# A hybrid decoder layer by Strassen-like products: attention's projection by columns, stores on ACT's queue, split weights stored later, and one more set of products by seven

## The chip, the cores and the metric

One Trainium2 chip, of which the kernel uses 1 core. The metric is the time of the launch on the device, in microseconds; lower is better. The core has five engines that work side by side, each through a queue of its own: PE (matmuls), DVE (vector), ACT (scalar, activations), POOL (GpSimd) and SP (here it only issues DMAs). Matrices lie in SBUF, sums of products in PSUM, of which a bank holds 128 x 512 numbers.

## The reference

One step of one layer: a sliding-window attention branch and a gated linear attention (GLA) branch in parallel, merged by gates, then an output projection and a layer norm. There are 2048 prompt tokens and 8 x 8 sample tokens; the model's width is 1024. All is float32.

```python
z = jnp.einsum('btd,dn->btn', x, w_in)
q, k, v, g_att, gq, gk, gv, g_gla, g_lr, r_att, r_gla = jnp.split(z, SPLIT_POINTS, axis=-1)
o_att = swa_prompt(q, k, v, attn_sink, rel_table)          # windows of 128, softmax with sinks
log_a = jax.nn.log_sigmoid(g_lr @ w_gk_up + b_gk) / GATE_NORMALIZER
o_gla, S = gla(gq * (GLA_HK ** -0.5), gk, gv, log_a, s0)   # recurrent state, chunk by chunk
o_gla = o_gla * lax.rsqrt(mean(o_gla ** 2) + EPS) * gla_norm_w
h_att = (o_att * silu(g_att)) @ w_pa
h_gla = (o_gla * silu(g_gla)) @ w_pg
merged = sigmoid(r_att) * h_att + sigmoid(r_gla) * h_gla
x = layer_norm(DN_ALPHA * x + merged @ w_o, ln_g, ln_b)
```

Besides y the kernel returns the last keys and values and the GLA states, for prompt and sample. It computes `sigmoid` by `tanh`, and the halves that this needs are folded into later steps.

## The kernel before, in words

**Float32 by parts.** A float32 product goes through PE as three products of a high and a low part: `wh*xh`, `wh*xl` and `wl*xh` (lines 1291, 1292, 1293). The parts are made by `split` (line 140): ACT casts the high part (L142), DVE subtracts it from the source to get the low part (L143).

**Products by seven.** The 2112 tokens are three thirds s of 704, and a third is two halves t of 352 columns. For a pair of 256 output columns (p) and the two halves of the depth (k), the four blocks of the output (two column halves c by two token halves t) come from seven block products in place of eight (Strassen's scheme in Winograd's form). The products have numbers, in the order 1, 7, 6, 4, 5, 2, 3 (`ORDER`); a product is one *group* of 12 matmuls of 352 columns. For it there are seven operands of x (`Ops`: x1 to x7, sums and differences by `mix`, parts by `make`) and seven weights (`w_make`). Where a weight's block is used for the first time, POOL adds and subtracts the raw blocks (L338) for weights 7, 6 and 3. Products 1, 7 and 6 are copied from PSUM by ACT into `a` tiles (L374, L378), and DVE adds these to products 4, 5 and 2 (L383, L389, L395).

**Sets.** The main loop runs over groups, set by set: x0, x1, a0, u0, x2, a1, u1, a2, u2. An x set is the input projection of a third (17 column pairs) and the two gates r (8 pairs, `RA_`, `RG_`). An a set is attention's projection of a third (`PA_`, weights `w_pa`, depth 512, so that a group is 6 matmuls), a u set is GLA's (`PG_`, weights `w_pg`). The sets named in `PLAIN` go by eight plain products, in 16 groups for two pairs, the others by seven, in 14. In a plain set two pairs have four PSUM banks (`role`), one for each pair and token half.

**Side work.** `tick` starts work of the attention, of GLA and of setup at given ticks of the main loop; its matmuls stand between the groups. Setup makes the relative bias (`setup0` to `setup5`); `gla_norm` has two small steps on POOL (L1071, L1072).

**Weights.** Ahead of group g the loop issues the load of raw weights of group g + 8 into `ws` tiles (`w_first`, L311, on SP), the load of kept weights of g + 5 (`w_kept`, L318), makes the weight of g + 4 (`w_make`, into `wp` tiles, of which there are six), and loads the gates `part` for g + 2 (L175). In x0 the made weights 7, 6, 5, 3 are stored to HBM (L361, `wk`), and x1 and x2 load them instead of making them anew.

**Sinks.** What is done with an output tile: `keep_sink` stores it (L187), `silu_sink` (L202) and `tanh_sink` (L212) apply an activation first, `gated_sink` of an a set multiplies it by its gate `part` on DVE (L219) and stores it (L221), `merge_sink` of a u set does the same (L227) and adds it to that in HBM by POOL's accumulating DMA (L229). All the other stores and loads are issued by SP.

**What sets the order.** PE's order is the program's. The other engines' orders are set when the kernel is built, largely by the order in the program; each engine then waits for what its next instruction needs, and so does SP with each DMA. Small tiles come from pools with a fixed number of buffers (`mtile`: `xb` 16, `a` 8, `fin` 10, `ws` 9, `wp` 6), and an instruction that writes a buffer waits until the earlier use is over.

Of the kernel before, what the change touches and what calls it, by code (L numbers as in the profile page):

```python
# [12 lines left out]
F32 = mybir.dt.float32  # L13
# [37 lines left out]
EIGHT = [(c, k, t) for c in range(2) for k in range(2) for t in range(2)]  # L51
PLAIN = ("a0", "a1", "a2", "u0", "u1", "u2")
KEPT = (7, 6, 5, 3)
# [4 lines left out]
def kernel(ctx, tc, io):  # L58
# [22 lines left out]
    def mtile(tag, dt=F32, name=None):  # L81
        n, bufs = {"xb": (4 * T, 16), "a": (T, 8), "fin": (T, 10), "ws": (512, 9), "wp": (D, 6)}[tag]
        pool = px if tag == "xb" else pr
        return pool.tile([P, n], dt, tag=tag, name=name or tag, bufs=bufs)
# [97 lines left out]
    def keep_sink(dst):  # L182
        def f(z, ps, parts, p, c, ts):
            if ps:
                z, src = mtile("fin"), z
                nc.scalar.copy(z, src)  # L186
            nc.sync.dma_start(dst[:, c, ts], z)  # L187
            wrote(dst, c, ts)
        return f
# [16 lines left out]
    def tanh_sink(dst):  # L206
        def f(z, ps, parts, p, c, ts):
            src = z
            if ps:
                z = mtile("fin")  # L210
            nc.scalar.activation(z, src, AF.Tanh, scale=0.5)
            nc.sync.dma_start(dst(2 * p + c, ts), z)  # L212
        return f
# [43 lines left out]
    for n, (kind, s, kh, prs) in enumerate(sets):  # L257
        start_of.append(len(groups))
        base.append(int(tk))
        for pr_ in prs:  # L260
            if not groups:
                for k, t in ((0, 0), (1, 0), (0, 1), (1, 1)):
                    for c in range(2):
                        for j, (q, p) in enumerate(pr_):
                            groups.append((n, q, (c, k, t), s, p, 4 * t + 2 * c + j, False))
            elif seq[n] in PLAIN:
                for c in range(2):
                    for k in range(2):
                        for j, (q, p) in enumerate(pr_):
                            for t in range(2):  # L270
                                groups.append((n, q, (c, k, t), s, p, role[2 * j + t], False))
            elif len(pr_) == 2:
                for i in ORDER:
                    for j, (q, p) in enumerate(pr_):
                        b = role[j] if i in (1, 6, 5, 3) else role[2 + j]
                        groups.append((n, q, i, s, p, b, True))
                role = role[2:] + role[:2]
            else:
                (q, p), = pr_
                r = [role[2], role[3], role[0], role[1]]  # L280
# [9 lines left out]

    raws, wps, acc, parts = {}, {}, {}, {}
    LR, LK, LM, LP = 8, 5, 4, 2
    BLK = {1: (0, 0), 7: (1, 0), 6: (1, 1), 2: (0, 1)}
# [7 lines left out]
    def w_first(g):  # L301
# [7 lines left out]
        if c is not None:  # L309
            t = mtile("ws")[:, :q.kh * P]  # L310
            nc.sync.dma_start(t, q.w[c[0], c[1], p])  # L311
            raws[q.name, p, c] = t
# [7 lines left out]
    def w_make(g):  # L320
# [38 lines left out]
        if i in KEPT and keeps(q, p, s):  # L359
            d = wk_d[q.name, p, i] = dram.tile([P, 2 * m], F32, name=f"wk_{q.name}{p}{i}")  # L360
            nc.sync.dma_start(d, w.bitcast(F32))  # L361

# [300 lines left out]
    def setup3():  # L663
        flat = bs_d.rearrange("h q j -> h (q j)")
        for kv in range(2):
            b = w4(name="bias").rearrange("p (g k) -> p g k", g=G)
            for g in range(G):
                f = flat[kv * G + g, 127:127 + P * (LB - 1)].rearrange("(q j) -> q j", j=LB - 1)
                nc.sync.dma_start(b[:, g, :], f[:, :2 * W])
            st1["bias", kv] = b  # L670
# [14 lines left out]

    at(17, later(setup0))
    for h in range(0, NH, 2):
        at(20 + h, later(lambda h=h: setup1(h)))
    at(20, later(setup2))
    at(29, later(setup4))  # L690
    at(34, setup5)

# [421 lines left out]
    def samp_a(B):  # L1114
# [151 lines left out]
    half = 0  # L1266
    last_ = start_of[U2] + 14
    NG = len(groups)
    for g, (n, q, i, s, p, b, ch) in enumerate(groups):
        if 8 <= g + LR < NG:  # L1270
            w_first(g + LR)
        if g + LK < NG:
            w_kept(g + LK)
        if 8 <= g + LM < NG:
            w_make(g + LM)
        if g + LP < NG:
            _, q_, i_, s_, p_, _, _ = groups[g + LP]
            parts[g + LP] = q_.partners(i_, p_, s_)
        xh, xl = ops[n].op[i[1:] if type(i) is tuple else i]
# [269 lines left out]
```

## Time and profile before

| what | value |
|---|---|
| median of 3 runs | 1842.92 us (1842.38 to 1844.45) |
| the profiled execution | 1844.21 us, span 1842.3 us |
| granted clock of PE, mean | 0.990 |
| PE busy | 1782.9 us, 97% of the span |
| DVE, ACT, POOL busy | 1062.9, 832.6, 336.1 us |
| moved by DMA | 452.03 MB, 245 GB/s on average |

A line like L311 is the line of the kernel before. `PEld` is the loading of a matmul's stationary part, which runs beside the matmuls. Busy times of PE overlap from one matmul to the next. A row of the waits names who waited, for whom, the sum in us, the number of times and the longest. SPq is SP's queue, on which DMAs are issued.

### The profile page before, as it was taken

The page shows a single profiled execution, that of the slowest core. Times are in us where ns is not written, and L with a number is a line of the kernel's source. Part 1 is how long each engine was busy: PE and PEld are TensorE (multiplying, and loading weights), DVE is VectorE, ACT ScalarE, POOL GpSimd, SP SyncE. Part 2 cuts the span into 40 slices and gives each one's busy share as a digit, 9 for nine tenths or more (in the row PEclk, how much of TensorE's full clock was granted, in tenths as well). Part 3 has the DMA queues.
Part 4 walks back from the last instruction along what each step waited for, and adds up shares of the span by engine and source line. Part 5 has one row for each costly group of instructions (what it writes and reads, how often), then busy time and mean ns, then how long its engine had stood idle before and what let it go on. Part 6 is the DMA issues. An engine that isn't in the chain of part 4 may idle for free.

```text
span 1842.3 us, 31141 instructions
## 1 busy us (share of the span) xinstructions
PE 1782.9 (97%) x10850; PEld 1659.2 (90%) x10850; DVE 1062.9 (58%) x2077; ACT 832.6 (45%) x1983; POOL 336.1 (18%) x473
## 2 busy tenths in 40 slices
PE   8989999998999999999899999999999999999997
PEld 7888988998898899999899998899999889998886
DVE  6568676767636554545566446545455544535665
ACT  5747554645835643545334645544445332311100
POOL 4333345454100000000033000000000022021111
PEclk9999999999999999999999999999999999999999
DMA  6689588887698779888886897689888987976531
GB/s 192 237 294 320 196 291 284 299 281 244 201 297 290 239 233 295 274 262 270 285 236 134 274 313 228 218 277 330 264 279 284 299 228 188 293 152 213 159 110 52
DMA packets 291340, 452.03 MB, mean 245 GB/s; under 512 B 29981, under 2 KB 210517, under 8 KB 291168
## 3 DMA queue, kind: packets, MB, share of 16 engines
q1 hardware_dynamic: 283264, 440.61, 72.6%
q0 software_dynamic: 7824, 9.31, 3.6%
q8 instruction: 86, 1.41, 0.3%
q14 instruction: 70, 0.57, 0.1%
q10 hardware_dynamic: 96, 0.13, 0.0%
HBM read 297.52 MB, written 153.30 MB: 245 GB/s over the span
## 4 chain that ended last, share of the span: by engine, by line
PE 71%; DMA 11%; ACT 6%; DVE 5%; issue 3%; POOL 3%; SPq 1%; DVEq 0%; ACTq 0%; POOLq 0%
PE pd L1291 16%; PE pd L1293 16%; PE pd L1292 16%; PE pd L1355 3%; PE pd L1354 3%; PE pd L1356 3%; DMA ws<-w_g 2%; POOL ws L338 2%; DMA r<-ug_d 2%; DVE wp L143 1%; DMA part<-ra_d 1%; PE pa L811 1%; PE pa L765 1%; PE pa L797 1%; PE pa L1085 1%
## 5 line engine op out<-in xcount | busy, mean ns | idle before, releaser
L143 DVE TENSOR_TENSOR wp<-ws,wp 128x512 fp32r<-128x512 f32 (+1 forms) x396 | 271.9, 691 | 216.4 <-ACT wp L142 207.8
L142 ACT CAST wp<-ws 128x512 fp32r<-128x512 f32 (+1 forms) x396 | 233.7, 595 | 222.0 <-PE pd L1293 145.0
L338 POOL TENSOR_TENSOR ws<-ws 128x256 f32<-128x256 f32 x162 | 140.6, 898 | 159.9 <-DVE wp L143 116.0
L1071 POOL TENSOR_SCALAR sq<-sq 128x1 f32<-128x1 f32 x68 | 22.6, 333 | 727.6 <-ACT on L1070 727.6
L374 ACT COPY m<-pd 128x352 f32<-128x352 f32 x146 | 65.6, 453 | 89.2 <-PE pd L1293 89.1
L1291 PE MATMUL pd<-x7h,wp 128*128 128x352 f32 x292 | 97.4, 334 | 4.0 <-ACT wp L142 2.4
L1355 PE MATMUL pd<-woh,x 128*128 128x512 f32 x256 | 100.0, 391 | 0.0
L1354 PE MATMUL pd<-woh,x 128*128 128x512 f32 x256 | 99.8, 390 | 0.0
L1356 PE MATMUL pd<-wol,x 128*128 128x512 f32 x256 | 99.5, 389 | 0.0
L1291 PE MATMUL pd<-x1h,wp 128*128 128x352 f32 x292 | 96.2, 329 | 2.9 <-ACT fin L186 2.3
L1291 PE MATMUL pd<-x2h,wp 128*128 128x352 f32 x292 | 98.7, 338 | 0.0
L1291 PE MATMUL pd<-x6h,wp 128*128 128x352 f32 x292 | 97.5, 334 | 0.9 <-ACT wp L142 0.9
L1291 PE MATMUL pd<-x3h,wp 128*128 128x352 f32 x292 | 97.1, 333 | 0.0
L1291 PE MATMUL pd<-x4h,wp 128*128 128x352 f32 x292 | 96.9, 332 | 0.0
L1291 PE MATMUL pd<-x5h,wp 128*128 128x352 f32 x292 | 96.9, 332 | 0.0
L1293 PE MATMUL pd<-x1h,wp 128*128 128x352 f32 x292 | 94.3, 323 | 1.8 <-DVE wp L143 1.8
L1293 PE MATMUL pd<-x7h,wp 128*128 128x352 f32 x292 | 94.4, 323 | 0.9 <-DVE wp L143 0.7
L1292 PE MATMUL pd<-x2l,wp 128*128 128x352 f32 x292 | 95.0, 325 | 0.0
L1293 PE MATMUL pd<-x5h,wp 128*128 128x352 f32 x292 | 94.9, 325 | 0.0
L1292 PE MATMUL pd<-x5l,wp 128*128 128x352 f32 x292 | 94.9, 325 | 0.0
L1293 PE MATMUL pd<-x2h,wp 128*128 128x352 f32 x292 | 94.7, 324 | 0.0
L1293 PE MATMUL pd<-x6h,wp 128*128 128x352 f32 x292 | 94.4, 323 | 0.1
(441 smaller groups left out, 5271.0 us busy)
## 6 DMA issues: line engine op xcount, KB each, us to landing
wp<-wk_w_g SPq DMA_DIRECT2D x96, 512.0 KB
ws<-w_g SPq DMA_DIRECT2D x120, 256.0 KB
wk_w_g<-wp SPq DMA_DIRECT2D x48, 512.0 KB
wp<-wk_w_ra SPq DMA_DIRECT2D x32, 512.0 KB
wp<-wk_w_rg SPq DMA_DIRECT2D x32, 512.0 KB
ws<-w_at SPq DMA_DIRECT2D x54, 256.0 KB
wp<-wk_w_at SPq DMA_DIRECT2D x24, 512.0 KB
ws<-w_pg SPq DMA_DIRECT2D x48, 256.0 KB
```

The lines of the kernel that those rows point to most:

```text
L142: pin["a"] = nc.scalar.copy(dst_h, src)
L143: i = eng.tensor_tensor(dst_l, src, dst_h.bitcast(F32), ALU.subtract)
L338: nc.gpsimd.tensor_tensor(o[:, c], x[:, c], y[:, c], op)
L374: nc.scalar.copy(A[i], ps)
L765: mm(ps[kv][:, j, k0:], A["zq"][r, g0 + j, :], A["kk"][r, 0, k0:], start=True, stop=True, tile_position=(kv * HD, 0))
L1071: nc.gpsimd.tensor_scalar(sq[:n], sq[:n], EPS, None, op0=ALU.add)
L1291: mm(ps, wh, xh[:, ts], start=first, stop=False, skip_group_check=ch)
L1292: mm(ps, wh, xl[:, ts], start=False, stop=False, skip_group_check=ch)
L1293: mm(ps, wl, xh[:, ts], start=False, stop=(k == q.kh - 1 and not (type(i) is tuple and i[1] == 0)), skip_group_check=ch)
L1354: mm(ps, xh[:, xs], hi, start=(k == 0), stop=False)
L1355: mm(ps, xl[:, xs], hi, start=False, stop=False)
L1356: mm(ps, xh[:, xs], lo, start=False, stop=(k == KT - 1))
```

## The change

It does these things at once.

- `u1` is no longer in `PLAIN`: GLA's projection of the second third goes by seven products.
- In a plain a set the loop over a pair's depth half k goes inside that over the pairs: a pair's two banks are completed before the other pair's are begun. The u sets keep their order.
- The gates of an a set (`part`) are loaded up to six groups ahead instead of two.
- `tanh_sink` always, and `keep_sink` where ACT copied the tile out of PSUM, store from ACT's queue instead of SP's.
- A split weight's store to `wk` is issued a group later than the weight is made, and behind the last raw load.
- Raw weights are loaded nine groups ahead instead of eight (`LR`). In x0 weights are made five groups ahead instead of four. `ws` has ten buffers instead of nine, `a` seven instead of eight.
- Setup starts four ticks earlier (`SU`). Each bias tile is loaded by one DMA in place of four. Three tiles of the sample's work come from the `fin` and `ws` pools.

```diff
-PLAIN = ("a0", "a1", "a2", "u0", "u1", "u2")
+PLAIN = ("a0", "a1", "a2", "u0", "u2")
...
-        n, bufs = {"xb": (4 * T, 16), "a": (T, 8), "fin": (T, 10), "ws": (512, 9), "wp": (D, 6)}[tag]
+        n, bufs = {"xb": (4 * T, 16), "a": (T, 7), "fin": (T, 10), "ws": (512, 10), "wp": (D, 6)}[tag]
...
-            nc.sync.dma_start(dst[:, c, ts], z)
+            (nc.scalar if ps else nc.sync).dma_start(dst[:, c, ts], z)
...
             nc.scalar.activation(z, src, AF.Tanh, scale=0.5)
-            nc.sync.dma_start(dst(2 * p + c, ts), z)
+            nc.scalar.dma_start(dst(2 * p + c, ts), z)
...
+                jk = [(j, k) for j in range(2) for k in range(2)]
                 for c in range(2):
-                    for k in range(2):
-                        for j, (q, p) in enumerate(pr_):
-                            for t in range(2):
-                                groups.append((n, q, (c, k, t), s, p, role[2 * j + t], False))
+                    for j, k in jk if kind == "a" else [(j, k) for k, j in jk]:
+                        q, p = pr_[j]
+                        for t in range(2):
+                            groups.append((n, q, (c, k, t), s, p, role[2 * j + t], False))
...
-    LR, LK, LM, LP = 8, 5, 4, 2
+    LR, LK, LM, LP = 9, 5, 4, 2
...
-            nc.sync.dma_start(t, q.w[c[0], c[1], p])
+            pin["r"] = nc.sync.dma_start(t, q.w[c[0], c[1], p])
...
-            nc.sync.dma_start(d, w.bitcast(F32))
+            late.setdefault(g - 3, []).append(lambda: nc.sync.dma_start(d, w.bitcast(F32)))
...
-            for g in range(G):
-                f = flat[kv * G + g, 127:127 + P * (LB - 1)].rearrange("(q j) -> q j", j=LB - 1)
-                nc.sync.dma_start(b[:, g, :], f[:, :2 * W])
+            f = flat[kv * G:(kv + 1) * G, 127:127 + P * (LB - 1)].rearrange("g (q j) -> q g j", j=LB - 1)
+            nc.sync.dma_start(b, f[:, :, :2 * W])
...
-    at(17, later(setup0))
+    at(SU, later(setup0))
...
-        SA["kv"] = mt("skv", 2 * NS, 1).rearrange("p (a t) -> p a t", a=2)
-        SA["kw"] = mt("kw", W, 1)
+        SA["kv"] = mtile("fin", name="skv")[:, :2 * NS].rearrange("p (a t) -> p a t", a=2)
+        SA["kw"] = mtile("fin", name="kw")[:, :W]
...
-        if 8 <= g + LM < NG:
-            w_make(g + LM)
-        if g + LP < NG:
-            _, q_, i_, s_, p_, _, _ = groups[g + LP]
-            parts[g + LP] = q_.partners(i_, p_, s_)
+        while nm < NG and nm <= g + (LM + 1 if groups[nm][3] == 0 and seq[groups[nm][0]] == "x0" else LM):
+            w_make(nm)
+            nm += 1
+        for f in late.pop(g, ()):
+            with tc.issue_after(pin["r"].ins):
+                f()
+        while nq < NG and nq <= g + (LP + 4 if groups[nq][1] is PA_ else LP):
+            _, q_, i_, s_, p_, _, _ = groups[nq]
+            parts[nq] = q_.partners(i_, p_, s_)
+            nq += 1
```

The instructions of the whole program change thus: PE 48 matmuls fewer (four groups), ACT 135 DMA issues more and SP as many fewer.

SP in x0, where the second GLA head's tiles are stored (`ws<-w_g` is a raw load, `wk_w_g` a store of a split weight, `z_gg`, `z_kq` stores of output tiles, `gin`, `zkq` loads for GLA's side work). Before:

```order
L311 DMA ws<-w_g 128x512
L361 DMA wk_w_g_2566<-wp 128x1024
L202 DMA z_gg_97<-fin 128x352
L311 DMA ws<-w_g 128x512
L361 DMA wk_w_g_2603<-wp 128x1024
L187 DMA z_kq_90<-fin 128x352
L992 DMA gin<-zg_d 128x256
L995 DMA zkq<-z_kq_88 128x2x256
L311 DMA ws<-w_g 128x512
```

Now:

```order
L312 DMA ws<-w_g 128x512
L202 DMA z_gg_97<-fin 128x352
L312 DMA ws<-w_g 128x512
L362 DMA wk_w_g_2545<-wp 128x1024
L187 DMA z_kq_90<-fin 128x352
L993 DMA gin<-zg_d 128x256
L996 DMA zkq<-z_kq_88 128x2x256
L312 DMA ws<-w_g 128x512
L362 DMA wk_w_g_2568<-wp 128x1024
```

Each store of a split weight stands one raw load later.

DVE in A0, where a pair's output tiles are taken from the banks (`pd_74` to `pd_77` are the four banks, L219 the gated sink, L143 low parts of weights). Before:

```order
L219 SCALAR_TENSOR_TENSOR fin<-part,pd_74 128x352
L219 SCALAR_TENSOR_TENSOR fin<-part,pd_75 128x352
L143 TENSOR_TENSOR wp<-ws,wp 128x256
L219 SCALAR_TENSOR_TENSOR fin<-part,pd_76 128x352
L143 TENSOR_TENSOR wp<-ws,wp 128x256
L219 SCALAR_TENSOR_TENSOR fin<-part,pd_77 128x352
```

Now:

```order
L219 SCALAR_TENSOR_TENSOR fin<-part,pd_74 128x352
L219 SCALAR_TENSOR_TENSOR fin<-part,pd_75 128x352
L1103 TENSOR_TENSOR sg<-pa,sg 128x2x128
L1064 COPY_PREDICATED aper_207<-cmask,pa 128x128
L143 TENSOR_TENSOR wp<-ws,wp 128x256 x2
L219 SCALAR_TENSOR_TENSOR fin<-part,pd_76 128x352
L219 SCALAR_TENSOR_TENSOR fin<-part,pd_77 128x352
```

The four sinks came together at the end of eight groups; now two come in the middle of the eight and two at their end, with other work between.

POOL at the start of U1 (`mg_d` is the accumulating store, `sq` are the small steps of GLA's norm, `w_17011` and `ws` sums of raw weights). Before:

```order
L229 DMA mg_d<-fin 128x352 x3
L1122 MEMSET qz 128x256
L229 DMA mg_d<-fin 128x352
L1071 TENSOR_SCALAR sq<-sq 128x1
L1072 TENSOR_TENSOR sq<-sq,mhalf 128x1
```

Now:

```order
L339 TENSOR_TENSOR ws<-ws 128x256 x2
L339 TENSOR_TENSOR w_17011<-ws 128x256 x2
L339 TENSOR_TENSOR ws<-ws 128x256 x4
L339 TENSOR_TENSOR w_17034<-ws 128x256 x2
L339 TENSOR_TENSOR ws<-ws 128x256 x2
L229 DMA mg_d<-fin 128x352
```

Ten sums of raw weights stand in POOL's queue ahead of an accumulating store, where before there were none.

More of the change, by code (lines that the diff above doesn't have):

```diff
@@ L288 @@
     XS = (X0, X1, X2)
-    raws, wps, acc, parts = {}, {}, {}, {}
-    LR, LK, LM, LP = 8, 5, 4, 2
+    raws, wps, acc, parts, late = {}, {}, {}, {}, {}
+    LR, LK, LM, LP = 9, 5, 4, 2
     BLK = {1: (0, 0), 7: (1, 0), 6: (1, 1), 2: (0, 1)}
@@ L612 @@
     wgk = const.tile([P, HK], F32, name="wgk")
+    SU = 13
     at(8, later(consts))
@@ L683, in setup5 @@
             nc.sync.dma_start(bias_s[32 * b:32 * b + 32], bias_s[:32])
-    at(17, later(setup0))
+    at(SU, later(setup0))
     for h in range(0, NH, 2):
[L688 to L691, printed above, removed]
+        at(SU + 3 + h, later(lambda h=h: setup1(h)))
+    at(SU + 3, later(setup2))
+    at(SU + 12, later(setup4))
+    at(SU + 17, setup5)
     def gate_load(B):
@@ L1124, in samp_a @@
             nc.vector.tensor_copy(qz[:, b, b % 4 * TS:(b % 4 + 1) * TS], B["q"][:, Tp + b * TS:Tp + (b + 1) * TS])
-        kz = mt("kz", 4 * HK, 1).rearrange("p (b k) -> p b k", b=4)
+        kz = mtile("ws", name="kz").rearrange("p (b k) -> p b k", b=4)
         nc.vector.tensor_tensor(kz, kdT.unsqueeze(1).broadcast_to([P, 4, HK]),
@@ L1266 @@
     half = 0
-    last_ = start_of[U2] + 14
+    nm, nq = 8, 0
     NG = len(groups)
```

## Prediction

> **What bounds the kernel now.** I read the page's head first, then one table of stretches cut where the loop goes from one set of products to the next, then the waits of PE and of SP's queue inside the stretches where PE is idle. The stretches, in order: set x0, x1, A0 (attention's projection of the first third of the tokens), A1, U1 (GLA's projection of the second third), A2, U2.
>
> ```profile
> span 1842.3 us, 31141 instructions
> PE 1782.9 (97%) x10850; PEld 1659.2 (90%) x10850; DVE 1062.9 (58%) x2077; ACT 832.6 (45%) x1983; POOL 336.1 (18%) x473
> ...
> core 0: us, PE busy (x) PEld busy (x) DVE busy (x) ACT busy (x) POOL busy (x), PEclk, DMA share, GB/s
> 46.20:461.00 414.80, 391.50 (x2367) 364.27 (x2366) 285.77 (x512) 238.48 (x576) 174.46 (x218) 0.98 0.79 272
> 461.00:878.00 417.00, 413.54 (x2618) 391.64 (x2617) 223.09 (x453) 219.35 (x541) 21.12 (x42) 1.00 0.81 263
> 878.00:923.60 45.60, 40.25 (x227) 38.68 (x226) 25.16 (x56) 15.79 (x38) 2.66 (x6) 0.93 0.89 287
> ...
> 1421.60:1464.00 42.40, 39.37 (x233) 37.82 (x232) 26.68 (x68) 17.04 (x44) 4.59 (x9) 0.96 0.94 303
> 1464.00:1545.40 81.40, 79.37 (x495) 74.37 (x493) 39.36 (x96) 25.67 (x59) 19.83 (x30) 1.00 0.79 213
> 1545.40:1588.20 42.80, 39.25 (x233) 34.79 (x232) 22.65 (x50) 13.08 (x29) 1.66 (x3) 0.96 0.86 262
> 1588.20:1649.50 61.30, 61.30 (x385) 61.30 (x385) 25.72 (x45) 14.94 (x25) 12.92 (x15) 1.00 0.82 213
> ```
>
> PE is the bound: 97% of the span. So a change pays in two ways only: fewer matmuls, or less of the little time in which PE stands. U2 is 385 matmuls of 352 columns in 61.3 us with PE never idle: 0.159 us each, my price for a matmul. PE stands for 414.8 - 391.5 = 23.3 us in x0, 5.4 in A0, 3.0 in A1, 2.0 in U1, 3.6 in A2, and 3.5 in x1. After a stop of some length the clock falls too, here after one of 2.45 us:
>
> ```profile
> 913.07 0.32 PE L1293 MATMUL pd<-x(0, 0)_9663,wp 128*128 128x352 f32 x1
> 915.84 0.43 PE L1291 MATMUL pd<-x(0, 1)_9705,wp 128*128 128x352 f32 x1 [2.45 <-DVE fin L219]
> ...
> 918.07 0.49 PE L1293 MATMUL pd<-x(1, 0)_9823,wp 128*128 128x352 f32 x1
> 918.36 0.49 PE L1291 MATMUL pd<-x(1, 1)_9868,wp 128*128 128x352 f32 x1
> ```
>
> From 918.07 to 918.36 a matmul takes 0.29 us instead of 0.16. By the granted clock in the table, the slow stretches cost 2% of 414.8 = 8.3 us in x0, 7% of 45.6 = 3.2 in A0, 1.7 in A1 and 1.7 in A2. That goes with the stops.
>
> **The change part by part. 1: U1 by seven products.** Two pairs of output columns went through 16 groups each, now 14: 4 groups of 12 matmuls fewer, 48 x 0.159 = -7.6 us of PE, on the path. In return it needs seven operands of x instead of four, seven weights instead of four, and sums:
>
> ```profile
> L143 DVE TENSOR_TENSOR x(1, 1)l<-r,x(1, 1)h 128x704 fp32r<-128x704 f32 x3 | 2.7, 890 | 2.3 <-ACT x(1, 1)h L142 2.3
> L143 DVE TENSOR_TENSOR wp<-ws,wp 128x512 fp32r<-128x512 f32 x348 | 251.9, 728 | 204.5 <-ACT wp L142 196.1 <-PE pd L1293 1.2 <-issue 0.9
> L338 POOL TENSOR_TENSOR ws<-ws 128x256 f32<-128x256 f32 x138 | 120.8, 902 | 153.5 <-DVE wp L143 109.6 <-DVE nm L775 25.8 <-DMA ws<-w_g 7.4
> L229 POOL DMA_DIRECT2D mg_d<-fin x15 | 13.5, 945 | 34.9 <-DVE fin L227 15.4 <-DVE asper L1119 8.3 <-DMA r<-ug_d 6.9
> ```
>
> DVE had 8 splits of 128x704 for U1; it gets 14 splits and 8 mixes, 14 more x 0.89 = 12.5 us. They are due by the start of U1, so they lie in A1, where DVE is busy 26.7 of 42.4 us: 39.2 afterwards, 92%. It fits (lower end 0), but DVE works in order and A1's sums on DVE free PE's banks, so some of it will be seen; the upper end is all of it, +12.5. I take +1.5, nearer the lower end, since x0 carries the same kind of work beside DVE at 286 of 415. In U1 itself come 12 more weight splits (12 x 0.73 = 8.7 us of DVE) and 12 sums, which 42 idle us of DVE hide. POOL gets 4 x 8 = 32 sums at 0.90 = 28.9 us, in one queue with the 16 accumulating stores at 0.95: 19.8 + 28.9 = 48.7 of 74 us. x0 has made weights on POOL that way for 11.5 pairs with 23.3 us of PE standing, 2.0 a pair for all causes: so 0 to +4 for two pairs; I take +1. Sum of 1: -5.1 (from -7.6 to +8.9).
>
> **2: A0, A1, A2 by columns, with attention's gates loaded earlier.** What stops PE there, and what is behind it in A0:
>
> ```profile
> PE pd L1291 <- DVE fin L219: 3.6, 2, 2.5
> PE pd L1291 <- ACT fin L211: 1.8, 1, 1.8
> ...
> PE pd L1291 <- DVE fin L219: 4.5, 4, 2.6
> ...
> 894.36 3.76 DMA part<-ra_d
> ...
> 899.14 4.93 DMA part<-ra_d
> ...
> 909.31 5.93 DMA part<-ra_d
> ```
>
> (The third row is the same wait in A1 to A2.) L219 takes a bank and a gate tile `part` to an output tile. The load of `part` takes 3.8 to 5.9 us and is issued two groups ahead, 2 x 6 x 0.159 = 1.9 us; the change issues it six groups ahead, 5.7 us. In the old order a bank is full in the fifth group of eight and taken again in the ninth, three groups (2.9 us) later; now it is full in the third and taken again in the ninth, five groups (4.8 us). Either step alone would cover a load of the middle size. The ceiling is 3.6 + 4.5 = 8.1 us of waits and 6.6 of slow clock, 14.7. The floor is 0: A0 already moves 287 GB/s and A1 303 with the DMA engines 89 and 94% busy, and an earlier issue makes no byte faster; the same bytes in 8 us less would need 13.1 MB in 38 us, 345 GB/s, more than any stretch above shows. What can wait past A0 is the weights and x of U0. I take half, -7, all from A0 and A2, since in A1 part 1 has filled DVE.
>
> **3: x0, where weights are made and stored.** PE's waits in x0, then SP's, then one case:
>
> ```profile
> PE pa L1085 <- DVE sg L1102: 4.1, 4, 2.4
> PE pd L1291 <- ACT wp L142: 4.0, 4, 1.4
> PE pa L1085 <- ACT gv L1053: 2.7, 1, 2.7
> PE pd L1293 <- DVE wp L143: 2.5, 2, 1.8
> PE pd L1291 <- ACT fin L186: 2.3, 1, 2.3
> PE pa L703 <- ACT brow L652: 2.1, 1, 2.1
> PE pa L751 <- DMA kk<-z_kv: 1.5, 1, 1.5
> ...
> SPq L361 <- DVE wp L143: 59.8, 37, 4.9
> SPq L212 <- ACT fin L211: 33.3, 17, 5.6
> ...
> 223.20 0.42 SPq L311 DMA_DIRECT2D ws<-w_g  x1
> 228.60 0.32 SPq L361 DMA_DIRECT2D wk_w_g<-wp  x1
> ...
> 233.19 0.59 SPq L311 DMA_DIRECT2D ws<-w_g  x1
> ...
> 238.07 7.47 POOL L338 TENSOR_TENSOR ws<-ws 128x256 f32<-128x256 f32 x8 [3.11 <-DMA ws<-w_g]
> ```
>
> SP stands 59.8 us before stores of split weights (L361) until DVE has made them, and 33.3 before stores of ACT's tiles; raw weights (L311) are queued behind. At 223.6 to 228.6 SP stands, the raw weight goes out at 233.19, POOL waits for it until 238.07, and PE stops for wp soon after. The change takes both out of SP's way (a store of a weight comes a group later, behind the raw load of the moment; ACT issues its own), loads raw weights nine groups ahead instead of eight and makes them five ahead instead of four. That answers the 4.0 + 2.5 us of waits for wp, which I count whole. Setup four ticks earlier and two loads of bias instead of eight answer brow and kk, 3.6 us, of which I count 2.5. The GLA waits (sg, gv, 6.8 us) have POOL and ACT behind them and stay. Of the 8.3 us of clock a third goes, 2.8. Together -11.8.
>
> Against it: 135 stores now cost ACT an issue, 49 in x0, 43 in x1 and 43 in x2. ACT's own DMAs in the trace:
>
> ```profile
> 1836.20 1.03 ACTq L1410 DMA_DIRECT2D o_y<-z  x2
> ```
>
> Two in 1.03 us, 0.52 each: 49 x 0.52 = 25 us in x0, on 238 of 415. Hidden (0), as long as ACT's idle time covers it; at the other end all 25 are seen. x0 now has one more group of 1.9 us between a weight's cast and its use, so I take +2. In x1 and x2 (22 us each, PE standing 3.5 us in x1) I take 0, because ACT has 198 us free there; behind that cover, the next thing to be late would be the cast of the next weight. A split weight's buffer comes back a group earlier in need and its store starts later, so four groups of 2.6 us (414.8 us over 161 groups) lie between store and reuse; loads and stores of the rows above took under 6 us, so nothing is added. One `a` buffer less, and small tiles put into `fin` and `ws`, are counted at 0: seven `a` buffers still hold the six of a pair. Sum of 3: -9.8.
>
> **The sum:** -5.1 - 7 - 9.8 = -21.9 us against the profiled execution of 1844.2 us, 1822.3. The runs' median is 1842.9, 1.3 below that execution: 1821.0.
>
> One page speaks against parts 2 and 3. The Trainium skill, "DMA: Bandwidth & Descriptors", section "Issuing engines are not separate DMA queues", says that DMAs of SP, ACT and GpSimd run on the same 16 engines and interleave, and that issuing from several only saves the sequencer's issue time. The trace agrees in so far as A1's 303 GB/s with 94% busy leave little to win; by that rule alone part 2 would be 0 and part 3 would be the issue time, and the second rival is what follows. I still take part 3, because the SP rows show time lost to waiting in the queue, not to bytes.
>
> **Rivals.** *Most stops in x0 go* (20%): the GLA stops too hang on POOL, which is blocked by the same raw loads; then x0 gives its 23.3 us and 8.3 of clock less a third, about -21, and the sum is -33: 1810, down to 1800. *Transfers bind* (20%): the loads come no sooner, A0 and A2 give 0 and x0 only the setup and some order, -3, U1 -5: -8, 1835. For it the 287 and 303 GB/s; against it x0's 272 with 79% busy. *ACT becomes the bound* (10%): the other side. Each store stands in ACT's queue ahead of a weight's cast or a bank's copy; 135 x 0.52 = 70 us, and it also waits there for its tanh to end. From 22 of these 70 us on PE's path the gain is gone; at half, 35, the kernel takes 1842.9 - 22 + 35 = 1856. For it: ACT ends waits for PE in x0 (4.0, 2.3, 2.7). Against it: it is 57% busy there. Smaller, inside the forecast: DVE in A1 gives back all of part 1 (+12.5 instead of 1.5), 1832.
>
> **How the numbers follow.** The forecast (50%) has its own range of 1812 to 1832. 80% is reached from 1800 (most of the first rival) to 1839 (all of the second, which may lose its setup gain); what is left out is a clear gain beyond 1800 and the third rival. A change under 0.2%, 3.7 us, can't be told from none. Faster: 0.50 + 0.20 + most of 0.20 less a little of the forecast = 0.85; same 0.06, out of the second rival; slower 0.09, the third.
>
> **What would show it.** U1 near 74 us with 336 matmuls and A1 still 41 to 45 with DVE over 85% busy (part 1); waits for L219 in A0 and A2 under 3 us together, and A0 near 41 us (part 2); x0 near 405 us, SP's waits at the store of wk under 20 us, ACT in x0 near 260 us (part 3). The prediction is wrong if A0 and A2 keep their length at 290 GB/s, if PE's waits for wp in x0 stay above 5 us, or if ACT's DMA issues appear ahead of PE's waits in the chain.

## The result: 1.1% faster, near the predicted time, by other amounts than predicted

The changed kernel takes 1824.6 us (median; 1823.5 to 1827.7) against 1844.5 us for the kernel before on the same chip: a ratio of 0.9889, 95% interval 0.9871 to 0.9907. The forecast was 1821.0. The profiled execution of the changed kernel took 1827.65 us, the longest of its five, against 1844.21 for that of before; 16.6 us are to be found in the two profiles. A few executions, here and in the experiments, ran at a granted clock of 0.56 to 0.65 and took 2475 to 2923 us; no time below counts them.

The head of the page after:

```profile
span 1825.6 us, 31092 instructions
PE 1769.3 (97%) x10802; PEld 1652.2 (91%) x10802; DVE 1089.1 (60%) x2115; ACT 850.3 (47%) x2013; POOL 371.2 (20%) x505
```

The stretches, cut as in the prediction where PE goes from one set of products to the next (here x0, x1, A0, U0, x2, A1, U1, A2). GLA's step for the samples, 26 matmuls, now stands between A1 and U1; it is counted to U1, inside which it stood before:

```profile
core 0: us, PE busy (x) PEld busy (x) DVE busy (x) ACT busy (x) POOL busy (x), PEclk, DMA share, GB/s
...
43.30:445.30 402.00, 385.23 (x2367) 363.77 (x2366) 283.61 (x513) 242.46 (x579) 175.50 (x218) 0.99 0.82 280
445.30:863.50 418.20, 414.31 (x2618) 392.89 (x2616) 220.99 (x451) 219.78 (x538) 21.22 (x42) 1.00 0.81 261
863.50:902.30 38.80, 37.24 (x228) 35.81 (x227) 23.29 (x54) 18.92 (x45) 2.37 (x6) 1.00 0.96 319
902.30:978.70 76.40, 74.39 (x458) 73.24 (x457) 45.42 (x82) 24.37 (x52) 25.89 (x37) 0.98 0.77 199
978.70:1407.70 429.00, 425.72 (x2805) 398.96 (x2804) 224.46 (x499) 217.49 (x531) 22.40 (x49) 1.00 0.82 266
1407.70:1447.80 40.10, 37.98 (x233) 36.27 (x232) 31.19 (x75) 17.69 (x47) 8.76 (x13) 1.00 0.88 278
1447.80:1529.00 81.20, 74.69 (x437) 68.45 (x436) 60.84 (x119) 38.04 (x87) 45.60 (x53) 0.96 0.77 201
1529.00:1571.40 42.40, 38.51 (x234) 35.10 (x233) 21.88 (x51) 9.95 (x24) 5.07 (x7) 0.96 0.94 290
```

Set against the rows of before: the setup ends 2.9 us earlier, x0 is 12.8 us shorter, A0 6.8, A1 2.3. U1 has 58 matmuls fewer in its row (437 against 495; some of these belong to GLA) and is as long as before: 81.2 against 81.4. U0 is 3.8 us longer and x2 3.6. So in their stretches parts 2 and 3 brought more than forecast and part 1 nothing at all.

PE stood 2.0 us of U1 before and stands 6.5 now. Its waits there now, then what ACT stood for the longest, now and (last row) before:

```profile
PE pa L1145 <- ACT on L1074: 2.2, 1, 2.2
PE pa L1062 <- DVE S L1092: 1.3, 1, 1.3
PE pa L1145 <- DVE sg L1103: 1.2, 1, 1.2
PE pa L1086 <- DVE sg L1103: 0.9, 1, 0.9
PE pa L1119 <- DVE sg L1103: 0.9, 1, 0.9
...
ACT on L1074 <- POOL sq L1073: 21.9, 6, 8.0
...
ACT on L1073 <- POOL sq L1072: 10.6, 7, 3.9
```

None of PE's waits is for a product's weight or operand. All are for GLA, whose matmuls stand between the products: its output `on`, its state `S`, its gated output `sg`. And ACT stands 21.9 us before one kind of instruction: L1074 scales GLA's output by 1/sqrt(mean square), and that factor comes from two steps on POOL of 128x1 elements, L1072 (add) and L1073 (power). The timeline of POOL and ACT shows why these are late (the last two rows are ACT's):

```profile
1473.00 1.43 POOL L339 TENSOR_TENSOR ws<-ws 128x256 f32<-128x256 f32 x2 [3.36 <-DVE wp L143]
1474.51 1.87 POOL L339 TENSOR_TENSOR w<-ws 128x256 f32<-128x256 f32 x2
1476.34 3.58 POOL L339 TENSOR_TENSOR ws<-ws 128x256 f32<-128x256 f32 x4
...
1482.92 0.93 POOL L229 DMA_DIRECT2D mg_d<-fin  x1
1483.63 0.50 POOL L1072 TENSOR_SCALAR sq<-sq 128x1 f32<-128x1 f32 x1
1484.22 0.57 POOL L1073 TENSOR_TENSOR sq<-sq,mhalf 128x1 f32<-128x1 f32 x1
...
1477.10 0.20 ACT L1071 ACTIVATION_READ_ACCUMULATOR on<-pa 128x1 f32 x1
1484.82 0.47 ACT L1074 ACTIVATE on<-pa,sq 128x256 f32<-128x256 f32 x1 [7.52 <-POOL sq L1073]
```

ACT has the sum of squares at 1477.3. POOL, in order, is inside a row of weight sums (L339) and reaches the small step at 1483.6. Until 1484.8 ACT does nothing, and the casts of weights, the copies of banks and the copy of gv behind it wait too. (Under "The change" I counted ten sums ahead of the store; the rows are twelve.)

PE's longest stop in U1 lies earlier, and there it is another instruction of ACT that POOL holds:

```profile
1448.04 9.70 POOL L339 TENSOR_TENSOR ws<-ws 128x256 f32<-128x256 f32 x8 [0.56 <-DMA ws<-w_pg]
...
1457.78 0.62 ACT L142 CAST wp<-ws 128x512 fp32r<-128x512 f32 x1 [3.19 <-POOL ws L339]
...
1459.88 0.47 ACT L1074 ACTIVATE on<-pa,sq 64x256 f32<-64x256 f32 x1 [1.11 <-POOL sq L1073]
```

A row of eight sums takes POOL 9.7 us. ACT stands 3.2 us before the cast of the weight that they make; the square, the norm and the scaling of the samples' output come behind this cast, and PE stops 2.2 us for it, until 1460.4. From 1457.8 to 1467.8 the granted clock is 0.66; 10 us at this clock are some 3.4 us lost (an estimate from these two numbers). So POOL's sums hold ACT in two ways: by the norm's small steps that stand behind them, and by the weights themselves.

### The profile page after: what moved, and what is told of

Its sections match the earlier page's. It is cut to its first block, busy times and chain, and to the rows that moved or that the text cites. A ratio compares the mean times of both kernels' runs of the same rounds, so it can differ in the third digit from the quotient of the medians.

```text
span 1825.6 us, 31092 instructions
## 1 busy us (share of the span) xinstructions
PE 1769.3 (97%) x10802; PEld 1652.2 (91%) x10802; DVE 1089.1 (60%) x2115; ACT 850.3 (47%) x2013; POOL 371.2 (20%) x505
## 5 line engine op out<-in xcount | busy, mean ns | idle before, releaser
L143 DVE TENSOR_TENSOR wp<-ws,wp 128x512 fp32r<-128x512 f32 (+1 forms) x404 | 277.3, 691 | 221.1 <-ACT wp L142 199.6
L339 POOL TENSOR_TENSOR ws<-ws 128x256 f32<-128x256 f32 x186 | 165.4, 925 | 168.0 <-DVE wp L143 103.4
L1072 POOL TENSOR_SCALAR sq<-sq 128x1 f32<-128x1 f32 x68 | 24.6, 361 | 704.4 <-ACT on L1071 704.4
L1297 PE MATMUL pd<-x7h,wp 128*128 128x352 f32 x308 | 103.6, 336 | 4.2 <-ACT fin L186 2.8
L1297 PE MATMUL pd<-x1h,wp 128*128 128x352 f32 x308 | 102.4, 333 | 1.0 <-ACT fin L186 1.0
L1297 PE MATMUL pd<-x2h,wp 128*128 128x352 f32 x308 | 103.4, 336 | 0.0
L1297 PE MATMUL pd<-x4h,wp 128*128 128x352 f32 x308 | 103.3, 335 | 0.0
L1297 PE MATMUL pd<-x6h,wp 128*128 128x352 f32 x308 | 102.8, 334 | 0.0
L1297 PE MATMUL pd<-x5h,wp 128*128 128x352 f32 x308 | 102.2, 332 | 0.0
L1299 PE MATMUL pd<-x7h,wp 128*128 128x352 f32 x308 | 100.1, 325 | 1.4 <-DVE wp L143 1.4
L1298 PE MATMUL pd<-x7l,wp 128*128 128x352 f32 x308 | 100.2, 325 | 0.0
L1299 PE MATMUL pd<-x5h,wp 128*128 128x352 f32 x308 | 100.2, 325 | 0.0
L1299 PE MATMUL pd<-x4h,wp 128*128 128x352 f32 x308 | 100.1, 325 | 0.0
L1299 PE MATMUL pd<-x1h,wp 128*128 128x352 f32 x308 | 99.9, 324 | 0.0
L1298 PE MATMUL pd<-x4l,wp 128*128 128x352 f32 x308 | 99.9, 324 | 0.0
L1298 PE MATMUL pd<-x1l,wp 128*128 128x352 f32 x308 | 99.9, 324 | 0.0
```

Source lines behind the costliest of these rows:

```text
L143: i = eng.tensor_tensor(dst_l, src, dst_h.bitcast(F32), ALU.subtract)
L339: nc.gpsimd.tensor_tensor(o[:, c], x[:, c], y[:, c], op)
L1072: nc.gpsimd.tensor_scalar(sq[:n], sq[:n], EPS, None, op0=ALU.add)
L1297: mm(ps, wh, xh[:, ts], start=first, stop=False, skip_group_check=ch)
L1298: mm(ps, wh, xl[:, ts], start=False, stop=False, skip_group_check=ch)
L1299: mm(ps, wl, xh[:, ts], start=False, stop=(k == q.kh - 1 and not (type(i) is tuple and i[1] == 0)), skip_group_check=ch)
```

## The experiments

Each kernel ran with the kernel before on the same chip; times are medians, ratios are to the kernel before. The reading that grew out of the profile: the 48 matmuls were given back because POOL's weight sums hold GLA's norm (called theory G, later P). The rival: DVE, with 14 more splits and 8 mixes, is short (D). A third reading came up later: GLA's last steps end too late for A2 and U2 (S).

**u1_plain** puts part 1 back.

```
-PLAIN = ("a0", "a1", "a2", "u0", "u2")
+PLAIN = ("a0", "a1", "a2", "u0", "u1", "u2")
```

> The changed kernel with U1 back at eight products a pair (part 1 undone: 48 matmuls more, no weight sums on POOL and no extra splits and mixes for U1). Theory G (the 48 matmuls were given back inside U1, since ACT waits there for POOL's small steps of GLA's norm, L1072 and L1073, behind the weight sums of L339): U1 stays 80 to 82 us, ACT's waits for sq in it fall from 21.9 us to about 10, and the time is within 3 us of the changed kernel's. As predicted (part 1 worth 5.1 us): U1 near 79 with no PE wait and A1 a little shorter, the time 4 to 6 us longer. Theory D (DVE's work for the seven operands is the price, paid in A1 and x2 too): A1 and x2 get shorter, x2 by 3 us, and the time is 2 to 5 us shorter than the changed kernel's.

1815.1 us, ratio 0.9862 (0.9839 to 0.9884): faster than the changed kernel by 9.5 us of median, by about 5 us in the ratios, whose intervals just overlap. So part 1 costs something like 5 to 10 us where 5.1 were forecast as a gain. Its profile, x2 to U1 and A2:

```profile
974.30:1399.60 425.30, 424.24 (x2797) 398.09 (x2797) 223.91 (x497) 217.43 (x531) 22.47 (x49) 1.00 0.82 267
...
1440.00:1522.80 82.80, 80.03 (x495) 75.59 (x493) 38.27 (x91) 24.49 (x57) 19.78 (x31) 0.98 0.76 202
1522.80:1559.20 36.40, 36.40 (x232) 33.51 (x231) 19.96 (x45) 10.53 (x24) 1.66 (x3) 1.00 0.96 296
```

U1 is 1.6 us longer, but x2 is 3.7 and A2 6.0 shorter, with no stop of PE in A2. The sign and x2 fit theory D; A1, which D wanted shorter, is as long as before (40.4 against 40.1), and A2 fits neither theory.

**norm_later** moves one ACT instruction.

```
-        nc.scalar.mul(on[:n], o, sq[:n])
...
+        f = lambda: nc.scalar.mul(on[:n], o, sq[:n])
+        if key == "s":
+            f()
+        else:
+            B["mul", key] = f
...
+    def gla_mul(B, i):
+        with tc.issue_after(pin["gv"].ins):
+            B["mul", i]()
...
+                    at(tt(u + i + 2) + 1, lambda B=B, i=i: gla_mul(B, i))
```

`pin["gv"]` is ACT's last copy of gv. The scaling for the samples (key "s") stays where it was.

> The changed kernel with one instruction moved on ACT: the scaling of GLA's output (L1074) stands behind the next copy of gv (4 to 9 ACT instructions later), so that ACT need not wait for POOL's two small steps. Nothing else is changed. Theory G: ACT's waits for sq go from 29.7 us in x0 and 21.9 in U1 to under 5 each, PE's standing in U1 falls from 6.5 us to under 2 (U1 74 to 77 us), GLA's stops in x0 (sg 4.2, gv 3.3, on 2.3) lose half: 7 to 14 us faster than the changed kernel. Theory D (DVE is what makes U1 late): the waits for sq go, U1 stays at 79 to 82 us and the time is within 3 us of the changed kernel's.

1820.2 us, ratio 0.9869 (0.9851 to 0.9888), 4.4 us less than the changed kernel by medians, with overlapping intervals. Its stretch U1:

```profile
1449.30:1523.00 73.70, 71.91 (x437) 67.27 (x436) 59.64 (x119) 36.21 (x82) 45.10 (x53) 0.98 0.80 215
```

U1 falls from 81.2 to 73.7 us with DVE as busy as before (59.6 us against 60.8): theory G holds for U1, D does not. PE stands 1.8 us there instead of 6.5, at one place: the samples' output, behind the cast that waits for POOL's sum. x0 is 2.6 us shorter. But x1 and x2 are 2 us longer each and A2 stays at 42.0, so the total gains less than the stretch, and less than the 7 to 14 us that G gave.

**a_old** undoes part 2 (`jk` as before for every set; LP + 4 back to LP).

> The changed kernel with part 2 undone: the A sets in the old order of groups and the gate parts loaded two groups ahead. By the stages of the profile (A0 -6.8, A1 -2.3, A2 -0.4, and U0 +3.8 given back): 5 to 6 us slower than the changed kernel, with U0 back at 72.6 us and no PE wait for S there. As predicted (7 us from A0 and A2): 7 us slower, with A2 longer too. Rival (the time only moves between neighbouring stages, since the same bytes have to come): within 2 us of the changed kernel.

1830.7 us, ratio 0.9934 (0.992 to 0.9949): part 2 is worth 6.1 us by medians. A0 is 43.1 us, A1 42.8 and A2 44.5 against 38.8, 40.1 and 42.4; U0 is 73.2. It is not a mere shift. The two steps of part 2, the order and the earlier gates, were undone together and are not told apart.

**sp_stores** puts ACT's 135 stores back on SP (`nc.sync.dma_start` in `keep_sink` and `tanh_sink`).

> The changed kernel with ACT's tiles stored from SP's queue again (135 DMA issues go from ACT to SP). If these stores were worth what the prediction put on SP's 33.3 us of standing: x0 4 to 8 us longer, SP's waits for ACT's fin back above 25 us in x0, POOL and PE waiting for raw weights again. If they are neutral (raw weights come nine groups ahead and the split weights' stores are out of the way): SP's waits come back, but x0 and the total stay within 2 us. If ACT's issues cost (0.52 us each): x0 to x2 together 3 us or more shorter.

1836.9 us, ratio 0.9957 (0.9943 to 0.9971): 12.2 us slower. x0 takes 414.1 us and SP stands 33.0 us for ACT's tiles (L212), so the first reading, and more than it asked. But POOL's waits for raw weights (w_g) in x0 did not come back: 17.3 us, against 20.8 in the changed kernel.

**gla_early** lets GLA end seven ticks sooner.

```
-        t1 = base[XS[s + 1]] + 30 if s < MS - 1 else base[U2] - 3
+        t1 = base[XS[s + 1]] + 30 if s < MS - 1 else base[U2] - 10
```

It was made because of this place in A2 of the changed kernel, ACT's row, DVE's row and PE's wait:

```profile
1563.23 0.78 ACT L142 CAST x(1, 1)h<-r 128x704 fp32r<-128x704 f32 x1 [6.71 <-DMA r<-ug_d]
...
1564.04 0.89 DVE L143 TENSOR_TENSOR x(1, 1)l<-r,x(1, 1)h 128x704 fp32r<-128x704 f32 x1 [4.67 <-ACT x(1, 1)h L142]
...
PE pd L1297 <- DVE fin L219: 3.9, 2, 2.4
```

GLA's last output is stored, loaded again as U2's x, cast by ACT and split by DVE; the gated sink L219 that frees PE's bank stands behind that split.

> The changed kernel with GLA's steps for the last third of the tokens spread up to ten ticks ahead of U2 in place of three (a tick is one group of 12 matmuls); nothing else is changed. U1 by seven is four ticks shorter, so the same GLA steps stand in less time. Theory S (the chain of GLA's last steps - POOL's norm, ACT, the store of sg, the load of U2's x, its cast on ACT, DVE's split - sets the end of U1 and A2, and not PE): the casts of U2's last x no longer stop ACT and DVE for 6.7 us in A2, A2 goes from 42.4 to 36 to 38 us, and U1 from 81 to 76 to 79: 6 to 10 us faster than the changed kernel, near 1815 to 1818. Rival P (POOL's weight sums alone make U1 late): A2 stays at 41 us or more, U1 stays at 80 or more, and the time is within 3 us of the changed kernel's.

1826.1 us, ratio 0.99 (0.9883 to 0.9918): no gain. U1 is 74.1 us and A2 39.7, but A1 grows from 40.1 to 53.6. Part of that is GLA's work on PE that has moved forward (267 matmuls in A1 for 233, and 197 in A2 for 234), and ACT's longest wait has moved with it; PE stops 6.8 us behind it:

```profile
ACT on L1074 <- POOL sq L1073: 16.6, 4, 11.5
```

**gla_early_norm** has both edits.

> Both: GLA's steps for the last third up to ten ticks ahead of U2, and the scaling of GLA's output behind the next copy of gv on ACT. If the two stops are separate causes: U1 near 74 us (norm_later had 73.7) and A2 at 36 to 38: 10 to 14 us faster than the changed kernel, 1810 to 1815, below the changed kernel with U1 back at eight products (1815.1). If moving the scaling only shifts the stop to the next bank of PE (waits for S, L1092): no better than the better of the two alone, 1815 to 1820.

1820.4 us, ratio 0.9875 (0.9855 to 0.9895): as norm_later alone. A2 is 36.6 us and U1 71.1, but A1 51.4, with an ACT wait of 10.5 us for POOL at the one norm that had not been moved (the samples'). In both kernels it is a row of twelve sums that stands ahead of this norm in POOL's queue. The stop goes where GLA's steps go, as long as POOL's sums stand there.

**sums_dve** takes U1's sums off POOL and keeps everything else.

```
+            if q.name == "w_pg":
+                add(o[:, :m], x[:, :m], y[:, :m], op)
+                return
             h = m // 2
```

> The changed kernel with the weight sums of U1 on DVE in place of POOL: 16 sums of 128x512 (about 0.7 us each, some 11 us of DVE) for POOL's 32 of 128x256 (29 us). U1 stays by seven. Theory P (POOL's sums hold GLA's two small norm steps, ACT waits for these, and the stop moves between A1, U1 and A2 with GLA's steps): ACT's waits for sq in U1 fall from 21.9 us to about 10, A1, U1 and A2 together go from 163.7 us to 152 to 157: 6 to 12 us faster than the changed kernel. Theory D (DVE is the one that is short, with 14 more splits and 8 mixes): 11 us more of DVE make A1, U1 and A2 longer, and the time is 3 to 10 us longer than the changed kernel's.

1810.6 us, ratio 0.9821 (0.9796 to 0.9847): 14.0 us faster than the changed kernel, and the fastest of all. The stretches A1, U1, A2, ACT's wait in U1, and DVE's sums:

```profile
1402.30:1441.80 39.50, 37.88 (x233) 36.24 (x232) 32.45 (x77) 19.24 (x51) 5.78 (x9) 1.00 0.88 276
1441.80:1512.00 70.20, 70.00 (x438) 65.65 (x438) 62.97 (x137) 37.07 (x85) 20.36 (x28) 1.00 0.91 243
1512.00:1554.40 42.40, 39.45 (x233) 36.28 (x233) 22.32 (x50) 11.43 (x26) 2.52 (x4) 0.92 0.93 285
...
ACT on L1077 <- POOL sq L1076: 15.0, 6, 4.5
...
L338 DVE TENSOR_TENSOR ws<-ws 128x512 f32<-128x512 f32 x12 | 8.2, 687 | 0.2
```

A1, U1 and A2 together take 152.1 us for 163.7. These 11.6 us are what the edit shows in its own stretches; the rest of the gain lies in stretches before these, which it does not touch. PE is busy 70.0 of 70.2 us in U1 with DVE 90% busy beside it. DVE was not short, it had room for another 11 us; what U1 lacked was room in POOL's queue. Of U1's 11.1 us, norm_later gets 7.5 by moving the scaling alone. The edit here also turns ACT's waits for POOL's sums before casts (6.6 us in U1) into 4.4 us for DVE's, and ends the slowing of DVE that is told at the end; how the other 3.6 us are divided between these is not shown. ACT's wait for the norm fell less than expected, to 15.0 us and not 10, but its longest from 8.0 to 4.5.

A sum of 128x512 takes DVE 0.69 us and takes POOL two steps of 0.89 (the mean in x0) to 1.03 (in U1 of the changed kernel). The Trainium skill, "GPSIMD Engine Reference", section "Engine selection", says to keep elementwise sums on VectorE, GPSIMD being about twice as slow for two inputs. The trace agrees where POOL works alone (33 of its sums have no instruction of DVE beside them, with a mean of 0.74 us: 2.1 times), and has 2.6 to 3 times beside DVE. The slowness alone was not the harm: POOL had time for the sums (45.6 of 81.2 us busy), but others waited behind them.

**norm_plain** is u1_plain with norm_later's edit.

> U1 back at eight products (1815.1 us) and the scaling of GLA's output behind the next copy of gv on ACT (4.4 us faster with U1 by seven). Theory P: with eight products POOL has no sums in U1, so the moved scaling helps only in x0 (2 to 3 us there) and at one stop of 2.8 us in U1: 2 to 6 us faster than with U1 at eight alone, 1809 to 1813. If moving the scaling costs as much elsewhere (x1 +2.2 us and x2 +1.9 in its profile): 1813 to 1817.

1818.5 us, ratio 0.9859 (0.9834 to 0.9883), against 1815.1 without the edit: nothing gained. x0 and U1 are some 4.6 us shorter each, x1 5.5 and A1 4.3 longer. Where POOL has no sums the moved scaling gains nothing overall; why x1 and A1 grow is not shown.

**before_act** gives the kernel before ACT's stores, and only these.

> The kernel before with one thing of part 3 alone: ACT stores its own tiles from its own queue (135 issues). The changed kernel with these stores back on SP was 12 us slower and its x0 was 414.1 us, as long as before. If the stores' queue alone brings the gain of x0: x0 402 to 406 us and 9 to 13 us faster than the kernel before. If it works only together with the later stores of split weights and the longer lead: x0 410 us or more, less than 5 us faster. As predicted (an issue costs ACT 0.52 us, 2 us of it seen in x0, 6 of its 11.8 us of gain due to SP's order): 3 to 6 us faster.

1835.4 us, ratio 0.9954 (0.9937 to 0.997), 9.1 us less than the kernel before by medians (8.5 by the ratio). The time fits the first reading, x0 does not: the profiled execution, 1839.7 us, is the longest of its six, and has x0 at 414.8 us, as long as before. Where the 9 us lie is not shown.

**rest_old** undoes the rest of part 3: the stores at once (as in stores_now, below), LR 8, LM 4 everywhere.

> The changed kernel with the rest of part 3 undone: split weights stored at once, raw weights loaded eight groups ahead, weights made four groups ahead; ACT's stores, the setup and the merged load of bias stay. If ACT's stores bring all of x0's gain: within 2 us of the changed kernel, x0 at 401 to 404 us. If the wp waits of PE (6.5 us before) are worth what the prediction counted: x0 6 to 8 us longer, PE's waits for wp in it back at 5 us or more. If the later stores only got in the way (SP still stands 63.2 us before them): 2 to 4 us faster.

1842.5 us, ratio 0.9987 (0.9976 to 0.9998): 17.9 us slower than the changed kernel. x0 is 414.0 us, 12.0 longer where 6 to 8 were expected, with 9.7 us of PE waits for wp (7.6 for its cast, 2.1 for its split).

**stores_now** undoes only the later stores.

```
-            late.setdefault(g - 3, []).append(lambda: nc.sync.dma_start(d, w.bitcast(F32)))
+            nc.sync.dma_start(d, w.bitcast(F32))
```

> The changed kernel with split weights stored at once again, and nothing else undone (the longer lead stays). With the shorter lead undone too it was 18 us slower and x0 12 us longer. If SP's queue order is what counts (a store that waits for DVE stands in front of the raw loads): SP's waits at this store rise from 63 to 80 us or more, POOL's waits for raw weights (w_g) in x0 from 21 to 35 us or more, x0 8 to 12 us longer. If the lead is what counts (nine groups for a load, five for making a weight): x0 within 3 us of 402, and the time within 4 us of the changed kernel's.

1834.0 us, ratio 0.9937 (0.9914 to 0.996): 9.4 us slower, x0 415.9 us. SP's wait before the stores, and POOL's waits for raw weights in x0:

```profile
SPq L362 <- DVE wp L143: 90.0, 45, 11.6
...
POOL w L339 <- DMA ws<-w_g: 23.1, 5, 8.1
POOL ws L339 <- DMA ws<-w_g: 12.1, 8, 3.7
```

In x0 of the changed kernel the same rows, and PE's waits, are:

```profile
SPq L362 <- DVE wp L143: 63.2, 29, 8.7
...
POOL w L339 <- DMA ws<-w_g: 11.2, 3, 6.4
POOL ws L339 <- DMA ws<-w_g: 9.6, 6, 2.7
...
PE pa L1086 <- DVE sg L1103: 4.2, 3, 2.8
PE pa L1086 <- ACT gv L1054: 3.3, 1, 3.3
PE pd L1297 <- ACT fin L186: 3.2, 2, 2.1
PE pa L1062 <- ACT on L1074: 2.3, 1, 2.3
PE pd L1299 <- DVE wp L143: 1.4, 1, 1.4
```

and in x0 of the kernel before POOL waited 35.1 us for w_g:

```profile
POOL w L338 <- DMA ws<-w_g: 27.7, 6, 7.1
...
POOL ws L338 <- DMA ws<-w_g: 7.4, 4, 3.1
```

35.1 us before, 20.8 after, 35.2 with the stores at once: the order in SP's queue decides when raw weights come. That alone does not set x0's length: sp_stores has 17.3 us of these waits and an x0 of 414.1. rest_old, without the longer lead too, is 8.5 us slower still, but not in x0 (414.0 against 415.9); no kernel here has only the lead undone.

**sums_dve_early** is sums_dve with gla_early's edit.

> U1's weight sums on DVE (1810.6 us) and GLA's steps for the last third up to ten ticks ahead of U2 in place of three. In A2 of the kernel with the sums on DVE, ACT waits 13.1 us for U2's last two blocks of x to come back from memory after GLA has stored them, DVE's splits wait behind, and A2 takes 42.4 us, against 36.5 with U1 at eight products, where GLA has four groups more. Theory S (GLA's last steps end too late for A2): A2 36 to 38 us, A1 and U1 together within 2 us of 109.7, 4 to 7 us faster: 1804 to 1807. Rival Q (GLA's earlier steps only move the stop forward, as in gla_early, where A1 grew by 13.5 us and POOL's norm stood 11.5 us behind the sums): A1 and U1 together 4 us or more longer, and the time 1809 to 1814.

1814.2 us, ratio 0.9842 (0.982 to 0.9863): 3.6 us slower than sums_dve by medians, with overlapping intervals: no gain. A2 falls from 42.4 to 37.7, A1 grows from 39.6 to 48.7. Some 5 to 6 us of that is PE work that has only moved (A2 196 matmuls for 233, A1 267 for 233), the rest a stop of 3.7 us for GLA's S. Rival Q fits; theory S, as I tried it, falls. The 6 us that A2 is longer with U1 by seven stay open.

By stretches, from each kernel's timeline (us; setup is the time up to the seventeenth group of x0):

| kernel | setup | x0 | x1 | A0 | U0 | x2 | A1 | U1 | A2 |
|---|---|---|---|---|---|---|---|---|---|
| before | 46.2 | 414.9 | 416.9 | 45.6 | 72.6 | 425.3 | 42.4 | 81.4 | 42.8 |
| after | 43.3 | 402.0 | 418.2 | 38.8 | 76.5 | 429.0 | 40.1 | 81.2 | 42.4 |
| u1_plain | 43.7 | 403.6 | 414.9 | 38.6 | 73.6 | 425.3 | 40.4 | 82.8 | 36.5 |
| sums_dve | 43.3 | 401.4 | 417.0 | 38.6 | 74.0 | 427.9 | 39.6 | 70.1 | 42.5 |
| sp_stores | 44.2 | 414.1 | 419.1 | 36.3 | 77.5 | 426.2 | 38.7 | 80.0 | 43.9 |
| rest_old | 43.7 | 414.0 | 419.3 | 37.3 | 74.8 | 428.4 | 39.8 | 83.0 | 44.5 |
| stores_now | 43.2 | 415.9 | 418.1 | 37.2 | 74.4 | 428.7 | 40.6 | 78.1 | 42.8 |

One caution on such a table: after, u1_plain and sums_dve issue the same instructions up to x2, and still have x1 at 418.2, 414.9 and 417.0 and U0 at 76.5, 73.6 and 74.0. A stretch of one profile is good to 2 or 3 us. Of U0's 3.8 us over before, a part may still be a price of part 2: without it U0 is 72.6 (before, before_act) and 73.2 (a_old), with it never under 73.4 in the kernels here. How much is not shown.

## Why the prediction was right, and where it was not

The time came out within 4 us because two errors cancelled: part 1 cost time where it was to gain 5, and part 3 gained more than forecast. That is luck; the sum was not sound.

**Part 1 was wrong**: -5.1 forecast, and undoing it gains 5 to 10 us. The step that failed is the term for POOL, "0 to +4 for two pairs; I take +1" (the "pairs" there are two pairs taken together; U1 has four). Moving just these sums to DVE gains 11.6 us in A1 to A2 and 14.0 by medians, so that was about their price. I had set POOL's 48.7 us of work against 74 us of time, and taken x0 as the example that it fits. The work was right (45.6 us busy in U1, with four sums already made in A1), but a sum of work says nothing of who waits behind it: GLA's two small norm steps stand in that queue as well, and ACT, in order, waits for these and for the weights that the sums make.

The term for DVE (+1.5) came out about right, its reason only in part. A1 is no longer than before (40.1 us, and 39.5 in sums_dve), but DVE is busy 31.2 us in it and not 39.2: six of the 14 splits lie in U1. The 48 matmuls are there too: with the sums on DVE, U1 is 12.7 us shorter than with eight products, of which 2.8 was a stop that u1_plain has there. Some 2.6 us are paid in x2 and 6 in A2. The 2.6 are no more than the scatter of one profile, but the kernels with U1 by seven have x2 at 426.2 to 430.9 us, and those with eight products at 425.3 to 426.8. sums_dve ends 4.5 us below u1_plain, close to the 5.1 that part 1 was to bring. The small rival "DVE in A1 gives back all of part 1" had the size right (12.5) and the engine wrong.

**Part 2 was right in sign, and about right in size**: -7 forecast, 6.1 by undoing it. With U1 at eight products the A sets together are 15.3 us shorter than before (7.0, 2.0 and 6.3), as much as the ceiling of 14.7; but these kernels differ by part 3 too, and none has part 2 undone with U1 at eight, so how much of the 15.3 is part 2's is not shown. The 6 us in A2 are lost when U1 goes by seven. The rival that transfers bind is refuted for A0: no L219 wait is left there, and it moves 319 GB/s at 96% busy, more than the 303 that I took as the most. For A2 it is not refuted: A2 keeps its length (42.8 and 42.4 us) at 290 GB/s with the DMA engines 94% busy, which is half of a sign that I had named for being wrong, and its waits for L219 are 3.9 us where "under 3" was for both sets.

**Part 3 was right in kind and too small**: -9.8 forecast, and setup and x0 alone are 15.7 us shorter. What was said to go went (waits for wp from 6.5 to 1.4 us, those for brow and kk from 3.6 to 0.2), and what was said to stay stayed (GLA's sg and gv, 6.8 before and 7.5 now). The forecast was 9.0 us less standing of PE, 2.8 of clock and 2 to pay for ACT's issues. Of x0's 12.8 us, 6.5 are less standing (23.3 to 16.8), and 6.3 are less busy time for the same 2367 matmuls (391.5 to 385.2); the setup gives 2.9 more. So the term for the clock was too small, and the price for ACT's issues isn't seen anywhere: an issue took ACT 0.33 us in the changed kernel and not 0.52, and the stores that cost ACT an issue are worth 12.2 us. Nor do the edits add up, which I had priced as separate, by their waits. x0 is 402 us with all of them, and 414 to 416 with only ACT's stores undone (sp_stores) or only the later stores undone (stores_now): undoing either takes back all of x0's gain. The case that I showed for SP was also less direct than it reads: SP issued another raw load at 229.48, and a store of a split weight, a store of a tile and two loads of GLA stand between that and the one at 233.19.

The rule that the prediction set against parts 2 and 3, from the Trainium skill, "DMA: Bandwidth & Descriptors", section "Issuing engines are not separate DMA queues", says that a second issuing engine saves issue time only. It does not cover the order in a queue: stores_now moves no issue to another engine, it only puts stores back ahead of loads on SP, and is 9.4 us slower.

**Of my marks, several were bad.** U1 "near 74" is 81.2, and DVE in A1 "over 85%" is 78%. "ACT in x0 near 260 us" could not come true, since ACT's column leaves out the instructions that issue its DMAs (it counts 579 after 576, with 49 issues more); it is 242.5. "SP's waits at the store of wk under 20" was wrong: they are 63.2. SP stands before that store as long as ever, but now with the raw load ahead of it instead of behind.

## What to carry to other kernels

Before work is added to an engine with room, list the small instructions already in its queue and who waits for each: POOL was busy 56% of U1, and still a step of 0.5 us came 6.3 us late behind a row of sums; an engine that waits in order passes the delay on. Time spent waiting in a queue is cut by putting what others need ahead of what waits; how long the queue stands is no measure of it. Edits that cure the same stop from several sides can't be priced by adding up the waits that each removes: here undoing either of two took back all of x0's gain. Try them undone singly from the whole.

## What the runs showed of the hardware that I had not expected

DVE and POOL slow each other where a DVE instruction takes two tensors from SBUF. In U1 of the changed kernel, where POOL makes its sums, and then in U1 of sums_dve, where it makes none, L227 has both tensors in SBUF, and L384 (L387 there) has one of them in PSUM (`pd`):

```profile
L227 DVE SCALAR_TENSOR_TENSOR fin<-part,fin 128x352 f32<-128x352 f32 x12 | 9.5, 794 | 0.2
L384 DVE TENSOR_TENSOR fin<-u,pd 128x352 f32<-128x352 f32 x4 | 2.1, 513 | 0.8 <-PE pd L1299 0.8
...
L227 DVE SCALAR_TENSOR_TENSOR fin<-part,fin 128x352 f32<-128x352 f32 x12 | 6.2, 519 | 0.0
...
L387 DVE TENSOR_TENSOR fin<-u,pd 128x352 f32<-128x352 f32 x4 | 2.1, 514 | 0.0
```

0.79 us beside the sums and 0.52 without them for the first, 0.51 in both for the second. Over the whole trace of the changed kernel, DVE's split of a 128x512 weight takes 0.69 us where no sum of POOL runs beside it and 0.97 where sums cover 70% of it or more; a sum of POOL takes 0.78 us with no such DVE instruction beside it and 1.00 with one. The Trainium skill, "SBUF — State Buffer", section "Who interferes with whom", says that a DVE instruction with two inputs in SBUF contends with a GpSimd instruction that reads SBUF; the rows agree. So the 8.2 us of sums that DVE makes in U1 of sums_dve raised its busy time there by 2.1 us only (60.8 to 63.0). This slowing was not what made U1 late in the main: in norm_later L227 is as slow (0.81 us), and U1 is 73.7 us.
